# Two-layer encoder trunk on one Trainium2 core: PSUM bank order, placing of the adaLN dots, of the norm products, and the pairing in the MLP head's second half

## The chip, the cores and the metric

The kernel runs on one core of one Trainium2 chip. The metric is device time in microseconds (us), as the median over runs. Engines go by the profile's names: PE (TensorE matmuls; PEld its weight loads), DVE (VectorE), ACT (ScalarE), POOL (GpSimd) and SP (SyncE, whose queue issues the transfers).

## What is computed

Two residual layers over x of shape (512, 1024). Each layer modulates an RMS norm by adaLN, runs a mixer, adds it back with a gate, and does the same with an MLP.

```python
for layer in range(DEPTH):
    mod = c_act @ ada_w[layer] + ada_b[layer]
    shift1, scale1, gate1, shift2, scale2, gate2 = jnp.split(mod[:, None, :], 6, axis=-1)
    h = rms_norm(x, norm_mix[layer]) * (1.0 + scale1) + shift1
    y = mixer_conv_hgrn(h, ...) if layer % 2 == 0 else mixer_stick_breaking(h, ...)
    x = x + gate1 * y
    h = rms_norm(x, norm_mlp[layer]) * (1.0 + scale2) + shift2
    x = x + gate2 * (jnp.square(jax.nn.relu(h @ mlp_w1[layer])) @ mlp_w2[layer])
```

The mixer of layer 0 is a gated convolution beside a gated linear recurrence (HGRN2); that of layer 1 is stick-breaking attention with 16 heads. D_MODEL is 1024, D_FF is 4096. `mod` is a product of one vector with a 1024 x 6144 matrix for each layer.

## The kernel before, in words

**Layout.** x is kept transposed, as eight tiles x0 to x7 of 128 features x 512 positions. A "half" is 256 positions (`H[0]`, `H[1]`).

**Products.** Every f32 weight tile (128 x 1024, 512 KB) is loaded by SP into `wraw` or `raw`, a ring of three buffers, then split into a high part `whi` (ACT, L271; in the planned stage L1365) and a low part `wlo` (DVE, L272; L1366). `whi` and `wlo` have four slots each. The input h is likewise kept as `hh` and `hl`, the MLP's hidden values as `hidh` and `hidl`. `mm3` (L281 to L283) then makes one triple of matmuls: whi x hh, whi x hl, wlo x hh. Eight triples, k = 0 to 7, make one output tile.

**adaLN dots.** `mod` isn't made on PE: `ada_piece` loads one 512 KB tile through the same ring of three buffers, and `ada_dot` (L420) is one DVE instruction that multiplies it with the broadcast c and sums each row into a column of `modr`. The elementwise product, which nobody reads, goes to a scratch tile `ascr` in bf16. Sixteen dots are made at the start; the other 80 wait in a list, `todo`, and `background(n)` takes the next n. Calls of it stand after the v and g products (4), after each of four `lin` products (2), in and after each of four convolutions (3 + 2), and in the blocks of the first MLP (`PIECES`: 3, 3, 3, 3, 2 for block 0, 3, 3, 2, 2, 2 for blocks 1 and 2, and 2 each for block 3, behind outputs 0 to 4).

**PSUM.** Up to the output projection of layer 0, pool `mps` holds `acc` (four banks), `lv` (two) and `misc` (two). Then it is closed, and pool `pp` has eight tiles b0 to b7 that take the banks over. `acc()` of that pool goes round them and begins with b4. A tag gets its place in the pool when it is first named, so before the change b4 lies on bank 0, b5 on bank 1 and so on round.

**Order of work in layer 0.** PE's order is the program's; the order of DVE, ACT and SP is set by the framework from priorities and estimated times. The output projection runs outputs 0 to 2 together, then 3, then 4 to 7 by halves. `x_add` (L506) adds an output to x, `nrm.add` adds the square to `nss`; the norm of a half (`finish`) sums `nss` and the last square over partitions by matmuls with a tile of ones (L497), takes the root (Ln, Exp and one Newton step on DVE) and writes eight h tiles, each by DVE, ACT, DVE (L466 to L468). Then comes the **MLP head** (`mlp_head`): hidden tiles 0 to 3 by halves. `first()` makes four outputs of half 0 with two banks (b4, b5), k outermost; `second(j)` makes half 1 one output after the other. `sums` prepares the inputs of the block products, on DVE and ACT. Four blocks follow, each with pairs of hidden tiles (`pair`), then outputs (`second`, `products`, `done`): 5 or 8 output tiles of eight triples each.

**Order of work from the end of MLP 0 to the head of MLP 1.** Here a planner (`Graph`) sets the order of PE, DVE, ACT and SP. Each operation has an estimated duration and a priority. The planner takes the earliest possible start, and among operations that can start then, the lowest priority number, then the one created first. Its engines start at time 0. Norm work has priority 0, triples and weight splits have 1. `finish` there (L1396) issues the sum by matmuls with ones (L1399), Ln and Exp (L1402, L1403), the Newton step (L1404 to L1406) and the h tiles (L1410 DVE, L1412 ACT, L1414 DVE). `NormTasks.add` makes the squares (ACT, L1385) and adds them to `nss` (DVE, L1389). All triples are held in the order of the list `order`. The three places with halves are: the tail of MLP 0 (outputs 5 to 7, 24 triples a half) followed by the q and k products of two head pairs (32 triples a half); and the last part of the attention's output projection (24 triples a half) followed by the head of MLP 1 (32 triples a half). `mean_squares` (L1452) sums the squares of q and k, which `q_evict` and `k_evict` make on ACT (L1426, L1443).

The choice of the planner, in its own words:

```python
t0 = min(t for t, o in at)
t, o = min(((t, o) for t, o in at if t <= t0 + self.tol), key=lambda c: (c[1].prio, c[1].seq))
```

Of the kernel before, what the change touches and what calls it, by code (L numbers as in the profile page):

```python
# [25 lines left out]
NT = 8  # L26
# [194 lines left out]
def trunk(tc, x_d, c_d, rep_d, small_d, const_d, ada_d, ws_d, win_d, wv_d, woab_d, w1_d, w2_d, wqk_d, wvc_d, woc_d, out_d):  # L221
# [53 lines left out]
    def load_w(src, of=None, at=AT512):  # L275
        return split_w(raw_w(src), of, at)
# [140 lines left out]
    def ada_dot(l, v, f, raw):  # L417
        scr = adap.tile([P, 1024], BF16, name="ascr", tag="ascr", bufs=1)
        col = l * 48 + v * 8 + f
        dve.tensor_tensor_reduce(out=scr, in0=raw, in1=cb, scale=1.0, scalar=0.0, op0=ALU.mult, op1=ALU.add,  # L420
                                 accum_out=modr[:, col:col + 1])
# [26 lines left out]
    def background(n):  # L448
        for _ in range(min(n, len(todo))):
            l, v, f = todo.pop(0)  # L450
            ada_piece(l, v, f)
            if f == 7:
                ada_done(l, v, 0, 8)
# [470 lines left out]
    for h in range(4):  # L924
        run(lin(h, do_hg, h))
        background(2)


    def conv(i):
# [19 lines left out]
        y[i] = (yh, yl)  # L949
        background(2)  # L950

# [21 lines left out]
    PLACES = {5: (mp, "F2", "Q2"), 6: (mp, "Ft", "Kt")}  # L973
    run(proj((0, 1, 2), [load_w(woab_d[o]) for o in (0, 1, 2)], FULL))
    for o in range(3, HALVED[0]):
        run(proj((o,), [load_w(woab_d[o])], FULL))
    ws = {o: load_w(woab_d[o], PLACES.get(o), AT256) for o in HALVED}
    for hf in range(2):
# [11 lines left out]

    pp = pool("pp", PSUM)

    bank = [4]
# [140 lines left out]

    PIECES = ((3, 3, 3, 3, 2), (3, 3, 2, 2, 2), (3, 3, 2, 2, 2), (2, 2, 2, 2, 2))

    def mlp(l, last, hp, head, th, more=()):
# [3 lines left out]
        for b in range(4):  # L1141
# [14 lines left out]
            def done(o, ps):  # L1156
                x_add(o, ps, FULL, l, GATE2)
                if b == 3:
                    if last:
                        sync.dma_start(out_d[o], x[o])  # L1160
                    else:
                        nrm.add(o, FULL)
                if o < 5:
                    background(PIECES[b][o])

            p0 = second(0)
            products(p0, 0, 7)
            rest()
            p1 = second(1)
            products(p1, 0, 7)  # L1170
# [26 lines left out]
    def mlp_head(l, nin, hp):  # L1197
# [21 lines left out]

        def second(j):  # L1220
            ps = acc(256)
            for k in range(NT):
                mm3(ps, w[j], ks(k), hT[k], H[1], k == 0, k == NT - 1)
                yield 0.32
            evict(j, ps, H[1])

        run(first())
        flush()
        more = []
        for j in range(4):  # L1230
            run(second(j))
            if j < 2:
                more.append(load_w(w1_d[l, 4 + j]))
            if j == 1:
                th = [[Handle(t=hp.tile([P, 1088], F32R, name=f"t{i}{a}", tag=f"t{i}{a}")[:, AT512]) for a in "hl"] for i in range(4)]
                sums(l, th, lambda eng, n, fn, r, w: fn())
# [156 lines left out]

    def finish(parts, hf, l, which, table, at=-9.0):

        sl, ps, a, y = H[hf], miscs.new(), nass.new(), nys.new()  # L1396

        for i, q in enumerate(parts):
            on_pe(0.44, lambda i=i, q=q: pe.matmul(ps.t[:, :256], ones, q.t[:, sl], start=(i == 0), stop=(i == len(parts) - 1)),  # L1399
                  (q,), (ps,), 0, at=at)  # L1400
        m = lambda: ps.t[:, :256]
# [223 lines left out]
    for hf in range(2):  # L1625
        for o in range(5, 8):
            order += [mm3h(tail[o, hf], whole, w_tail[o - 5], ks(k), (hid[k],), H[hf], k == 0, k == 7, 256) for k in range(8)]
            on_dve(310, lambda o=o, hf=hf: x_add(o, tail[o, hf].t, H[hf], 0, GATE2), (tail[o, hf], xh[o, hf]), (xh[o, hf],), 0)
            nt_.add(o, hf)
        if hf:  # L1630
            gate = G.op("HOST", 0.0, open_attention, after=[order[-1]])
            for r in ap_rings:
                r.gate = gate
        finish([nt_.acc[hf]] + [nt_.sq[o, hf] for o in nin.direct], hf, 1, 0, ())
    w = [weights(wqk_d[s // 2, s % 2], None, AT256) for s in range(4)]
    for hf in range(2):
        ps = [r.new() for r in (accs, accs, zts, zts)]
        for k, s in by_half(hf, 4):
# [23 lines left out]
    nt_ = NormTasks((5, 6, 7))  # L1662
    for hf in range(2):
        order += wout(2, hf, wl, nt_)
        if hf == 0:
            hh = h_parts([[ring(base, [P, T], F32R, f"h{a}{i}").new() for a in "hl"] for i in range(NT)])
        finish([nt_.acc[hf]] + [nt_.sq[o, hf] for o in nt_.direct], hf, 1, 1, table)

# [24 lines left out]

    w = [weights(w1_d[1, j], None, AT256) for j in range(4)]
    for hf, sl in enumerate(H):

        ps = [accs.new() for _ in range(2)] if hf == 0 else [zts.new() for _ in range(4)]
        ps = [(ps[j // 2], lambda t_, j=j: t_[:, H[j % 2]]) if hf == 0 else (ps[j], half) for j in range(4)]
        for k, j in by_half(hf, 4):
            order.append(mm3h(*ps[j], w[j], ks(k), (hh[hf][k],), sl, k == 0 and (hf == 1 or j % 2 == 0), k == NT - 1, 256))  # L1700
# [94 lines left out]
```

## Time and profile before

| | |
|---|---|
| median of three runs | 1259.93 us (1259.74 to 1262.07) |
| the profiled execution, its own time | 1268.89 us |
| its span | 1267.1 us |
| mean granted PE clock | 0.986 |
| busy: PE / DVE / ACT | 1231.2 / 891.7 / 619.1 us |
| read from HBM | 155.96 MB |

The profile is one execution. Busy times are unions of instructions on an engine. A row of the timeline gives start, length, engine, line, what is written from what, and in brackets the idle time before it with what ended that. A granted clock below 1 in a stretch means that for a part of it PE ran at a lower clock; (1 - clock) x length is the time lost if PE had work throughout.

### The profile page before, as it was taken

The numbers are of one execution on the slowest core, as the hardware profiler recorded it, in microseconds if no ns is written. First come the engines' busy times: TensorE is split into PE (matmuls) and PEld (weight loads), VectorE is DVE, ScalarE is ACT, GpSimd is POOL, SyncE is SP. The second block draws the span as 40 slices with busy tenths as digits, with TensorE's granted clock in tenths as the row PEclk, the third lists the DMA queues.
The fourth block names the chain that finished last, engine by engine and source line by source line (L and its number), as shares of the span: only waits on it lengthen the run. The fifth ranks groups of instructions, "written<-read, shape, count | busy, mean of one in ns | idle before, by whom it ended". The sixth has DMA issues, their size and how long they took to land.

```text
span 1267.1 us, 19222 instructions
## 1 busy us (share of the span) xinstructions
PE 1231.2 (97%) x7649; PEld 1066.7 (84%) x7649; DVE 891.7 (70%) x1435; ACT 619.1 (49%) x1111; POOL 13.8 (1%) x24
## 2 busy tenths in 40 slices
PE   8999999999999999999999999999989999999998
PEld 6788777889779799798878787778888898898998
DVE  8897777659768787787657774668786574675661
ACT  4333133337238256264447763667565274372560
POOL 0000000000000000000120000000000000000000
PEclk9999899999999999999989999999989999999999
DMA  8666544312743735626413212231113224243141
GB/s 302 243 212 216 165 166 134 133 35 89 253 140 126 255 119 177 222 98 219 167 37 97 84 51 83 85 100 67 51 47 104 100 85 132 67 148 102 51 151 50
DMA packets 46618, 163.50 MB, mean 129 GB/s; under 512 B 5296, under 2 KB 6328, under 8 KB 46528
## 3 DMA queue, kind: packets, MB, share of 16 engines
q1 hardware_dynamic: 46384, 161.78, 38.7%
q8 instruction: 60, 0.98, 0.3%
q10 hardware_dynamic: 144, 0.49, 0.1%
q14 instruction: 30, 0.25, 0.1%
HBM read 155.96 MB, written 2.10 MB: 125 GB/s over the span
## 4 chain that ended last, share of the span: by engine, by line
PE 73%; DVE 11%; DMA 9%; ACT 4%; issue 2%; SPq 0%; ACTq 0%; DVEq 0%
PE b L281 17%; PE b L283 17%; PE b L282 17%; DMA wraw<-in_w 4%; PE acc L281 3%; PE acc L282 3%; PE acc L283 3%; DVE wlo L272 3%; DVE ascr L420 2%; DMA wraw<-in_ada 2%; ACT whi L271 2%; PE b L1532 1%; PE b L1553 1%; PE b L1588 1%; PE b L1452 1%
## 5 line engine op out<-in xcount | busy, mean ns | idle before, releaser
L271 ACT CAST whi<-wraw 128x1024 fp32r<-128x1024 f32 x125 | 130.2, 1049 | 235.0 <-DMA wraw<-in_w 78.0
L281 PE MATMUL b<-hidh,whi 128*128 128x512 f32 (+1 forms) x560 | 210.3, 376 | 4.4 <-ACT whi L271 4.4
L283 PE MATMUL b<-hidh,wlo 128*128 128x512 f32 (+1 forms) x560 | 210.0, 375 | 2.4 <-DVE wlo L272 2.4
L282 PE MATMUL b<-hidl,whi 128*128 128x512 f32 (+1 forms) x560 | 209.4, 374 | 0.0
L281 PE MATMUL b<-hh,whi 128*128 128x256 f32 (+1 forms) x632 | 198.3, 314 | 3.6 <-DVE x L506 2.9
L272 DVE TENSOR_TENSOR wlo<-wraw,whi 128x1024 fp32r<-128x1024 f32 x125 | 152.0, 1221 | 60.9 <-ACT whi L271 59.1
L283 PE MATMUL b<-hh,wlo 128*128 128x256 f32 (+1 forms) x632 | 193.6, 306 | 0.3 <-DVE wlo L272 0.3
L282 PE MATMUL b<-hl,whi 128*128 128x256 f32 (+1 forms) x632 | 193.2, 306 | 0.0
L281 PEld LDWEIGHTS b<-hh,whi 128*128 128x128 f32 x632 | 120.8, 191 | 16.3 <-issue 7.2
L281 PEld LDWEIGHTS b<-hidh,whi 128*128 128x128 f32 x560 | 106.3, 190 | 24.0 <-ACT whi L271 6.1
L506 DVE SCALAR_TENSOR_TENSOR x<-b,modc,x 128x512 f32<-128x512 f32 (+1 forms) x102 | 67.9, 673 | 83.1 <-PE b L283 82.9
L282 PEld LDWEIGHTS b<-hl,whi 128*128 128x128 f32 x632 | 122.6, 194 | 4.5
L283 PEld LDWEIGHTS b<-hidh,wlo 128*128 128x128 f32 x560 | 106.0, 189 | 24.1 <-DVE wlo L272 5.4
L283 PEld LDWEIGHTS b<-hh,wlo 128*128 128x128 f32 x632 | 120.9, 191 | 5.8 <-DVE wlo L272 0.5
L282 PEld LDWEIGHTS b<-hidl,whi 128*128 128x128 f32 x560 | 106.5, 190 | 18.4 <-DVE hidl L291 0.3
L420 DVE CUSTOM_DVE_ANT_0 ascr<-wraw,cb 128x1024 bf16<-128x1024 f32 x80 | 97.8, 1222 | 27.2 <-DMA wraw<-in_ada 26.5
L272 DVE TENSOR_TENSOR wlo<-tt,whi 128x1024 fp32r<-128x1024 f32 x52 | 63.3, 1220 | 28.6 <-ACT whi L271 28.0
L271 ACT CAST whi<-tt 128x1024 fp32r<-128x1024 f32 x52 | 53.4, 1050 | 44.1 <-PE b L282 30.4
L1366 DVE TENSOR_TENSOR wlo<-raw,whi 128x1024 fp32r<-128x1024 f32 x34 | 41.5, 1221 | 24.7 <-ACT whi L1365 24.5
L291 DVE TENSOR_TENSOR hidl<-cm,hidh 128x256 fp32r<-128x256 f32 (+1 forms) x90 | 44.5, 509 | 17.1 <-ACT hidh L290 16.1
L281 PE MATMUL acc<-hh,whi 128*128 128x512 f32 x128 | 53.2, 416 | 0.0
L282 PE MATMUL acc<-hl,whi 128*128 128x512 f32 x128 | 50.9, 398 | 0.0
(378 smaller groups left out, 2642.4 us busy)
## 6 DMA issues: line engine op xcount, KB each, us to landing
wraw<-in_w SPq DMA_DIRECT2D x124, 512.0 KB, 3.7
wraw<-in_ada SPq DMA_DIRECT2D x80, 512.0 KB, 4.4
eraw<-in_ada SPq DMA_DIRECT2D x16, 512.0 KB, 4.1
wraw<-in_win SPq DMA_DIRECT2D x16, 512.0 KB, 4.2
raw<-in_wqk SPq DMA_DIRECT2D x16, 512.0 KB, 3.7
raw<-in_ws SPq DMA_DIRECT2D x8, 512.0 KB, 6.9
wraw<-in_woab SPq DMA_DIRECT2D x8, 512.0 KB, 3.3
raw<-in_wvc SPq DMA_DIRECT2D x8, 512.0 KB, 4.3
```

What stands on the lines that cost most here:

```text
L271: act.copy(hi, raw)
L272: dve.tensor_tensor(lo, raw, hi.bitcast(F32), op=ALU.subtract)
L281: pe.matmul(ps, whi, h[0][:, hs], start=start, stop=False, **kw)
L282: pe.matmul(ps, whi, h[1][:, hs], start=False, stop=False, **kw)
L283: pe.matmul(ps, wlo, h[0][:, hs], start=False, stop=stop, **kw)
L291: dve.tensor_tensor(lo[:, sl], t_[:, sl], hi[:, sl].bitcast(F32), op=ALU.subtract)
L420: dve.tensor_tensor_reduce(out=scr, in0=raw, in1=cb, scale=1.0, scalar=0.0, op0=ALU.mult, op1=ALU.add, accum_out=modr[:, col:col + 1])
L506: dve.scalar_tensor_tensor(x[o][:, sl], ps, mcol(l, v, o), x[o][:, sl], op0=ALU.mult, op1=ALU.add)
L1366: on_dve(1024, lambda: dve.tensor_tensor(lo.t, raw.t, hi.t.bitcast(F32), op=ALU.subtract), (raw, hi), (lo,), 1)
L1452: on_pe(0.13, lambda s=s, sq=sqs[p, s, s0]: pe.matmul(ms.t[64 + 32 * s:96 + 32 * s, sl], hs, sq.t[:, sl], start=True, stop=True), (sqs[p, ...
L1532: pe.transpose(tp.t[:, o_:o_ + P], be.t[:, w0:w0 + P], ident)
L1553: pe.matmul(po.t[orow, P * b - t0:P * (b + 1) - t0], v.t[:, c, hcol], be.t[:, w0:w0 + P], start=first[j], stop=(c == b), skip_group_check= ...
```

## The change

Five edits.

1. `ada_dot` writes its product over the weight tile itself; the scratch tile `ascr` is gone.
2. The 80 dots are placed anew: one instead of two after each `lin` product and after each convolution, two each at three places around the first four outputs of the output projection, two in the MLP head, and `PIECES` in six entries of 2 or 3, the first of which stands between the first and the second output weight of a block.
3. b0 to b7 are named in order when pool `pp` is opened, so b4 lies on bank 4.
4. The head's second half makes two outputs at a time, in both layers.
5. In the planner, `finish` is created later, and its first matmul waits for a set triple of `order` (ninth of the second half, sixth of the second half, or ninth of what follows).

```diff
     def ada_dot(l, v, f, raw):
-        scr = adap.tile([P, 1024], BF16, name="ascr", tag="ascr", bufs=1)
         col = l * 48 + v * 8 + f
-        dve.tensor_tensor_reduce(out=scr, in0=raw, in1=cb, scale=1.0, scalar=0.0, op0=ALU.mult, op1=ALU.add,
+        dve.tensor_tensor_reduce(out=raw, in0=raw, in1=cb, scale=1.0, scalar=0.0, op0=ALU.mult, op1=ALU.add,
                                  accum_out=modr[:, col:col + 1])
...
         run(lin(h, do_hg, h))
-        background(2)
+        background(1)
...
         y[i] = (yh, yl)
-        background(2)
+        background(1)
...
-    run(proj((0, 1, 2), [load_w(woab_d[o]) for o in (0, 1, 2)], FULL))
+    w = [load_w(woab_d[o]) for o in (0, 1, 2)]
+    background(2)
+    run(proj((0, 1, 2), w, FULL))
+    background(2)
     for o in range(3, HALVED[0]):
         run(proj((o,), [load_w(woab_d[o])], FULL))
+        background(2)
...
     pp = pool("pp", PSUM)
+    for b in range(8):
+        pp.tile([P, T], F32, name=f"b{b}", tag=f"b{b}")
...
-    PIECES = ((3, 3, 3, 3, 2), (3, 3, 2, 2, 2), (3, 3, 2, 2, 2), (2, 2, 2, 2, 2))
+    PIECES = ((2, 2, 3, 2, 2, 2), (2, 2, 3, 2, 2, 2), (2, 2, 2, 2, 2, 2), (2, 2, 2, 2, 2))
...
-                if o < 5:
+                if 0 < o < len(PIECES[b]):
                     background(PIECES[b][o])
...
             products(p0, 0, 7)
             rest()
+            background(PIECES[b][0])
             p1 = second(1)
...
-        def second(j):
-            ps = acc(256)
+        def second(js):
+            ps = [acc(256) for _ in js]
             for k in range(NT):
-                mm3(ps, w[j], ks(k), hT[k], H[1], k == 0, k == NT - 1)
-                yield 0.32
-            evict(j, ps, H[1])
+                for p_, j in zip(ps, js):
+                    mm3(p_, w[j], ks(k), hT[k], H[1], k == 0, k == NT - 1)
+                yield 0.64
+            for p_, j in zip(ps, js):
+                evict(j, p_, H[1])
 
         run(first())
+        background(2)
         flush()
-        more = []
-        for j in range(4):
-            run(second(j))
-            if j < 2:
-                more.append(load_w(w1_d[l, 4 + j]))
-            if j == 1:
+        for js in ((0, 1), (2, 3)):
+            run(second(js))
+            if 0 in js:
+                more = [load_w(w1_d[l, j]) for j in (4, 5)]
...
-    def finish(parts, hf, l, which, table, at=-9.0):
+    def finish(parts, hf, l, which, table, after=()):
...
-                  (q,), (ps,), 0, at=at)
+                  (q,), (ps,), 0, after=after if i == 0 else ())
...
-        if hf:
-            gate = G.op("HOST", 0.0, open_attention, after=[order[-1]])
-            for r in ap_rings:
-                r.gate = gate
-        finish([nt_.acc[hf]] + [nt_.sq[o, hf] for o in nin.direct], hf, 1, 0, ())
+    gate = G.op("HOST", 0.0, open_attention, after=[order[-1]])
+    for r in ap_rings:
+        r.gate = gate
+
+    finish([nt_.acc[0]] + [nt_.sq[o, 0] for o in nin.direct], 0, 1, 0, (), [order[24 + 8]])
     w = [weights(wqk_d[s // 2, s % 2], None, AT256) for s in range(4)]
     for hf in range(2):
+        if hf:
+            finish([nt_.acc[1]] + [nt_.sq[o, 1] for o in nin.direct], 1, 1, 0, (), [order[48 + 8]])
...
-    for hf in range(2):
-        order += wout(2, hf, wl, nt_)
-        if hf == 0:
-            hh = h_parts([[ring(base, [P, T], F32R, f"h{a}{i}").new() for a in "hl"] for i in range(NT)])
-        finish([nt_.acc[hf]] + [nt_.sq[o, hf] for o in nt_.direct], hf, 1, 1, table)
+    order += wout(2, 0, wl, nt_)
+    hh, at = h_parts([[ring(base, [P, T], F32R, f"h{a}{i}").new() for a in "hl"] for i in range(NT)]), len(order)
+    order += wout(2, 1, wl, nt_)
+    finish([nt_.acc[0]] + [nt_.sq[o, 0] for o in nt_.direct], 0, 1, 1, table, [order[at + 5]])
...
-    w = [weights(w1_d[1, j], None, AT256) for j in range(4)]
+    w, at = [weights(w1_d[1, j], None, AT256) for j in range(4)], len(order)
     for hf, sl in enumerate(H):
+        if hf:
+            finish([nt_.acc[1]] + [nt_.sq[o, 1] for o in nt_.direct], 1, 1, 1, (), [order[at + 8]])
...
-        for k, j in by_half(hf, 4):
+
+        for k, j in by_half(0, 4) if hf == 0 else [(k, j) for js in ((0, 1), (2, 3)) for k in range(NT) for j in js]:
             order.append(mm3h(*ps[j], w[j], ks(k), (hh[hf][k],), sl, k == 0 and (hf == 1 or j % 2 == 0), k == NT - 1, 256))
```

## The prediction, made before the result was known

> **What bounds the kernel now.** I read the page first, for the engine that the span hangs on.
>
> ```profile
> span 1267.1 us, 19222 instructions
> PE 1231.2 (97%) x7649; PEld 1066.7 (84%) x7649; DVE 891.7 (70%) x1435; ACT 619.1 (49%) x1111; POOL 13.8 (1%) x24
> PEclk9999899999999999999989999999989999999999
> ```
>
> TensorE is busy for 97%, so an edit pays only where PE stands still or runs at a lower granted clock. I looked for such places in the busy times by stretch. Columns: stretch, its length, busy time of PE, PEld, DVE, ACT and POOL, granted clock, DMA share, GB/s.
>
> ```profile
> 143.00:154.00 11.00, 9.20 (x39) 7.60 (x38) 9.78 (x17) 1.04 (x1) 0.00 (x0) 0.69 0.52 161
> 225.00:250.00 25.00, 25.00 (x122) 21.10 (x121) 15.26 (x18) 11.57 (x13) 0.00 (x0) 1.00 0.43 147
> 271.00:280.00 9.00, 5.86 (x31) 5.23 (x31) 4.86 (x11) 2.78 (x6) 0.00 (x0) 0.81 0.18 58
> 280.00:310.00 30.00, 30.00 (x215) 28.23 (x213) 28.66 (x54) 22.93 (x47) 0.00 (x0) 1.00 0.15 44
> 335.00:360.00 25.00, 20.58 (x79) 15.24 (x78) 16.02 (x21) 6.29 (x6) 0.00 (x0) 0.93 0.73 243
> 432.00:436.00 4.00, 3.21 (x14) 2.02 (x13) 2.37 (x3) 1.05 (x1) 0.00 (x0) 1.00 0.62 217
> 518.00:522.00 4.00, 2.47 (x10) 1.39 (x10) 2.55 (x4) 1.04 (x1) 0.00 (x0) 1.00 0.45 154
> 617.00:625.00 8.00, 5.08 (x28) 4.70 (x27) 3.04 (x6) 1.96 (x4) 0.00 (x0) 0.79 0.43 136
> 643.00:660.00 17.00, 14.01 (x64) 10.41 (x64) 9.77 (x24) 9.20 (x24) 0.00 (x0) 0.70 0.05 11
> 917.00:929.00 12.00, 7.42 (x39) 6.53 (x39) 8.22 (x20) 4.49 (x11) 0.00 (x0) 0.72 0.14 44
> ```
>
> Each row gives two losses: length less PE busy, and (1 - clock) x length. They are 1.8 + 3.4 us at 143, 3.1 + 1.7 at 271, 4.4 + 1.8 at 335, 0.8 at 432, 1.5 at 518, 2.9 + 1.7 at 617, 3.0 + 5.1 at 643 and 4.6 + 3.4 at 917: together 39 us, 22 of idle time and 17 of clock. That is nearly all that this change can win. The rows 225:250 and 280:310 show none.
>
> [...]
>
> **The change part by part.** Two prices are used throughout: the pace of the three-matmul products.
>
> ```profile
> 236.01 0.39 PE L281 MATMUL acc<-yy,whi 128*128 128x512 f32 x1
> 236.69 0.39 PE L281 MATMUL acc<-yy,whi 128*128 128x512 f32 x1
> 617.27 0.28 PE L283 MATMUL b<-hidh,wlo 128*128 128x256 f32 x1
> 617.63 0.28 PE L283 MATMUL b<-hidh,wlo 128*128 128x256 f32 x1
> ```
>
> A triple of 512 columns takes 0.68 us and one of 256 takes 0.36, so an output tile of eight triples takes 5.4 or 2.8 us.
>
> *Dots in place* (L420). The instruction keeps its place and inputs; its output becomes f32 and overwrites the weight tile.
>
> ```profile
> L420 DVE CUSTOM_DVE_ANT_0 ascr<-wraw,cb 128x1024 bf16<-128x1024 f32 x14 | 17.1, 1221 | 2.6 <-DMA wraw<-in_ada 2.4
> L272 DVE TENSOR_TENSOR wlo<-wraw,whi 128x1024 fp32r<-128x1024 f32 x5 | 6.1, 1225 | 6.4 <-ACT whi L271 6.4
> L271 ACT CAST whi<-wraw 128x1024 fp32r<-128x1024 f32 x5 | 5.3, 1051 | 20.3 <-DMA wraw<-in_w 18.4 <-PE b L282 1.9
> wraw<-in_ada SPq DMA_DIRECT2D x14, 512.0 KB, 4.4
> wraw<-in_w SPq DMA_DIRECT2D x7, 512.0 KB, 4.7
> ```
>
> (Groups and DMA issues of 308 to 350.) The bf16 dot takes 1221 ns, a subtraction with a full-width output 1225. Cost 0; even 4 ns on all 80 dots is 0.3 us, beside PE.
>
> *Dots, ahead of the first MLP.* Two instead of one, fewer by eight up to the last convolution; six more behind the output projections, two in the head.
>
> ```profile
> 142.38 1.23 DVE L420 CUSTOM_DVE_ANT_0 ascr<-wraw,cb 128x1024 bf16<-128x1024 f32 x1 [2.24 <-DMA wraw<-in_ada]
> 145.49 0.74 PE L808 MATMUL lv<-Q,Kt 128*128 128x64 f32 x5 [1.80 <-DVE Kt L839]
> ```
>
> At 143 PE waits for a DVE product that stands behind a dot, and that dot waited 2.24 us for its transfer. With 24 dots instead of 32 in this stage, the three weight buffers come round sooner. The loss is 5.2 us; I take 4.2 as won (bounds 0 and 5.2), nearer to the upper end because one dot less at 1.2 us plus its transfer nearly covers the 2.24. The six moved dots (7.3 us of DVE and their six transfers on SP) lie under the 25 us of 225:250, where PE never waits, DVE has 9.7 us free and DMA is 0.43 busy; cost 0. Without that cover they would cost up to their 7.3 us. The two in the head land where DVE is full (28.66 of 30): I charge 0.5 us, with bounds 0 (they fit ahead of 281, where the 271 row has DVE idle for 4.1 of 9) and 2.4 (both delay the weight splits behind them one for one).
>
> *Dots of the four MLP blocks.* From 308 to 350, 14 + 7 tiles pass through three buffers in 42 us: 2.0 us a tile. Before, six dots stand between the second and third output weight, 12 us of queue, then three per output: four tiles, 8.0 us, against 5.4 us of products. That is the stall at 335, with ACT idle for 18.4 us on weight transfers. Now two dots go in ahead of the second weight and two to three follow each: three tiles are 6.0 us. The deficit per output falls from 2.6 to 0.6 us over five outputs, and the third weight's queue shortens by four tiles, 8 us. So the 6.2 + 0.8 + 1.5 = 8.5 us go but for 1.0: 7.5 won (bounds 4 and 8.5). Queued behind the earlier dots is the second weight itself, by 4 us; before it comes the whole seven-triple run on the first, 4.8 us.
>
> *Banks named in order* (b0 to b7 on banks 0 to 7). The head's first two accumulators leave the projection's banks.
>
> ```profile
> 271.13 1.05 ACT L271 CAST whi<-wraw 128x1024 fp32r<-128x1024 f32 x1
> 274.65 1.21 DVE L272 TENSOR_TENSOR wlo<-wraw,whi 128x1024 fp32r<-128x1024 f32 x1
> 274.78 0.39 PE L281 MATMUL b<-hh,whi 128*128 128x256 f32 x1 [2.86 <-DVE x L506]
> 275.91 0.38 PE L283 MATMUL b<-hh,wlo 128*128 128x256 f32 x1 [0.27 <-DVE wlo L272]
> ```
>
> The 2.86 us wait on `x` (L506) disappears. But the fourth head weight's low half is ready only at 275.9, DVE working through the norm before it, and the fourth product of k = 0 needs it. PE would run one more triple and wait for that. Won: 0 (upper bound 4.8, the row's loss; a loss has no mechanism, since the new banks are long free).
>
> *Head's second half by two.* The same 32 triples; each k lasts 0.7 us instead of 0.36, so the last tile of h is asked for 2.5 us later. PE has no idle time in 280:310, so nothing is won; the pairwise evictions come at most 2.8 us later, and the casts of the next weights with them, ahead of a use 5.6 us on. Cost 0 (bounds -0.3 and 0.5).
>
> *Norm products behind a set number of others.* Three places. The planner takes, of ready operations, the lower priority and then the earlier created; `finish` is now created behind the second half's additions to x, so these also go ahead of its h tiles on DVE.
>
> ```profile
> 617.84 1.23 DVE L1366 TENSOR_TENSOR wlo<-raw,whi 128x1024 fp32r<-128x1024 f32 x1 [0.67 <-ACT whi L1365]
> 620.34 0.43 DVE L1389 TENSOR_TENSOR nss<-nss,nsq 128x256 f32<-128x256 f32 x1 [0.54 <-ACT nsq L1385]
> 620.82 1.12 PE L1399 MATMUL b<-nss,ones 128*128 128x256 f32 x2 [2.92 <-DVE nss L1389]
> 629.50 1.67 DVE L1410 SCALAR_TENSOR_TENSOR tt<-x,gsc,ny 128x256 f32<-128x256 f32 x4
> 635.85 0.41 DVE L1389 TENSOR_TENSOR nss<-nss,nsq 128x256 f32<-128x256 f32 x1
> 646.22 0.39 ACT L1443 ACTIVATE nsq<-b 128x256 f32<-128x256 f32 x1
> 646.67 0.90 PE L1452 MATMUL b<-nsq,cons 128*32 128x256 f32 x4 [2.24 <-ACT nsq L1443]
> ```
>
> At 617.9 one triple of the first half is left. Ten triples, 3.6 us, now come before the sum, so PE reaches it at 621.5, behind 620.8. Won: 2.9 + 1.7 less 0.5 for the first h tile, about 4.1 (bounds 0 and 4.6). The sum's chain then starts some 3 us earlier against PE. Queued behind the sum's matmul is the rest of the tail; it no longer stands.
>
> At 643, PE waits for evictions that share ACT with the second half's h tiles. These were late because the second sum stood behind eight pairs of h instructions (629.5 to 635.9) on DVE. With the additions first, that sum can go behind nine projection triples, some 4 us earlier against PE; the h tiles (eight times 0.8 us) end about when the first half's 32 triples (11.4 us) do. Of 8.1 us I take 7.0 (bounds 0 and 8.1).
>
> ```profile
> 912.72 1.05 ACT L1365 CAST whi<-raw 128x1024 fp32r<-128x1024 f32 x1 [0.21 <-PE b L282]
> 921.10 0.41 DVE L1389 TENSOR_TENSOR nss<-nss,nsq 128x256 f32<-128x256 f32 x1
> 923.84 1.19 PE L1399 MATMUL b<-nss,ones 128*128 128x256 f32 x2 [4.58 <-DVE nss L1389]
> 924.01 1.21 DVE L1366 TENSOR_TENSOR wlo<-raw,whi 128x1024 fp32r<-128x1024 f32 x1
> ```
>
> At 917 the sum comes off PE's way, but behind it stands the same kind of split as in layer 0: the fourth weight's low half, of lower priority than all the norm's work on DVE, ends at 925.2. The fourth triple needs it. Won: 1.0 (bounds 0 and 8.0).
>
> **Sum**: 4.2 + 7.5 + 0 + 4.1 + 7.0 + 1.0 - 0.5 = 23.3 us. The profiled execution took 1268.89 us (span 1267.1 and 1.8 around it), so 1245.6. The median of the three runs is 1259.93, 0.7% less; the same share off gives 1236.8, so 1237.
>
> **The rivals.**
> 1. *The fourth weight is split early* (chance 0.16). Its cast is done at 913.8, in the gaps of the norm's short chain; a planner that takes the earliest start may slip it in there. Then 917 gives 7 us more and, likewise, 271 up to 4.8: 1225 to 1230. Against it: both rows show it last.
> 2. *The sums still block PE* (0.15). The plan starts DVE at time 0, but in the trace it was still splitting at 617.84; if `nss` is really later than planned, PE stands at the set place instead. The 11.1 us of 617 and 643 are lost: 1248.
> 3. *The clock dips stay* (0.07), having another cause than idle time. Only idle time is won: about 12 us, 1248. Every dip in the rows lies on idle time, which speaks against it. [...]
> 4. *Dots only trade places* (0.03), the transfers as late as now at 143 and 335 and the norms as in 2: under 1 us, 1259.5, no change.
> 5. *Slower* (0.07). [...]
>
> **How the numbers follow.** The forecast has 0.52, with a range of its own of 1230 to 1246. Faster by over 0.2% (2.5 us, about what a measurement of this kernel tells from no change): forecast and rivals 1 to 3, 0.90. Same 0.03, slower 0.07. The range from 1224 to 1253 takes in rivals 1 to 3 and the bounds of the MLP term, and leaves out the last two.
>
> **What would show it.** PE waits on `nss` gone or under 1 us in all; no granted clock below 0.9 around 617 and 643; the wait on `x` (L506) replaced by one on `wlo` (L272) of like length; ACT's wait for `in_w` transfers in the first MLP block under 8 us; no wait of PE on `Kt`. I am wrong if 271 or 917 become free of loss (rival 1), or if PE waits on `nss` at 621 or 631 for more than 2 us (rival 2).

## The result, and the profile after

The changed kernel takes 1246.03 us in the median, the kernel before beside it 1260.08 us: a ratio of 0.9883, with a 95% interval of 0.9864 to 0.9902. The 1246.03 is the median of four executions, one of which was slow (1502.91 us at a mean clock of 0.75); the other three took 1245.21, 1245.68 and 1246.37 us. Compared once more, the changed kernel took 1245.42 us, with the kernel before at 1264.02 beside it: a ratio of 0.9856 (0.9833 to 0.988). It is faster by 14 to 19 us in the medians. The forecast of 1237 lies 9 us too low, within its range of 1224 to 1253.

The two ratios are of one and the same kernel and differ by 0.0027, which is 3.4 us. So where two runs below differ by no more than that, their times don't settle which is faster; what an edit does at its place is then read from the traces.

The profiled execution of the changed kernel took 1245.21 us. The page, as for the kernel before:

```profile
span 1243.4 us, 19173 instructions
PE 1217.4 (98%) x7649; PEld 1058.9 (85%) x7649; DVE 890.5 (72%) x1435; ACT 618.7 (50%) x1111; POOL 11.2 (1%) x24
PEclk9999999999999999999999999999999999999999
```

All three slices at 8 are gone, and PE is busy for 13.8 us less with the same 7649 matmuls: fewer of them ran at a lower clock (its mean is 0.996, where it was 0.986). From profile to profile the span falls by 23.7 us, which is almost the forecast's 23.3; the medians differ by 14. The experiments settle what lies between.

The same stretches of work in the changed kernel, by the busy times in stretches (columns as in the prediction). The times have moved with the gain; the order is that of 143, 271, 335, 432, 518, 617, 643, the head of MLP 1 and its end.

```profile
141.00:152.00 11.00, 11.00 (x73) 9.86 (x71) 10.67 (x19) 2.28 (x3) 0.10 (x1) 1.00 0.34 108
264.00:273.00 9.00, 5.81 (x31) 5.28 (x30) 4.54 (x10) 2.69 (x6) 0.00 (x0) 0.81 0.17 58
327.00:345.00 18.00, 18.00 (x82) 14.88 (x80) 13.28 (x21) 3.16 (x3) 0.00 (x0) 1.00 0.74 239
416.00:420.00 4.00, 4.00 (x20) 3.30 (x19) 1.92 (x4) 0.00 (x0) 0.00 (x0) 1.00 0.80 252
500.00:504.00 4.00, 4.00 (x19) 3.30 (x19) 2.31 (x5) 1.05 (x1) 0.00 (x0) 1.00 0.86 294
598.00:606.00 8.00, 8.00 (x67) 7.89 (x66) 5.67 (x10) 5.51 (x10) 0.00 (x0) 1.00 0.42 137
621.00:638.00 17.00, 16.78 (x113) 12.47 (x111) 9.84 (x27) 10.98 (x28) 0.00 (x0) 1.00 0.32 91
889.00:901.00 12.00, 9.37 (x58) 8.77 (x57) 8.03 (x21) 5.13 (x13) 0.00 (x0) 0.86 0.02 8
917.00:929.00 12.00, 8.04 (x38) 6.53 (x38) 9.03 (x13) 5.86 (x11) 0.00 (x0) 0.86 0.26 88
```

Five of the nine rows are now full and a sixth (621) is so but for 0.2 us, all six at full clock. The row at 264 is as bad as it was, and the head of MLP 1 has two bad rows where it had one. PE's waits over the whole span name the tiles:

```profile
PE b L283 <- DVE wlo L272: 7.1, 2, 4.0
PE acc L651 <- ACT hh L640: 3.3, 3, 2.3
PE b L281 <- ACT hh L1419: 2.0, 1, 2.0
...
PE b L282 <- DVE hl L1421: 1.2, 2, 0.7
...
PE lv L807 <- DVE Kt L838: 1.0, 2, 0.5
...
PE b L281 <- DVE x L505: 0.2, 1, 0.2
```

No wait on `nss` is left (7.5 us before). The waits on `wlo`, 3.2 and 4.0 us, and on the `hh` of L1419 with the `hl` behind it are the new ends of the line (the `hh` of L640 belongs to the kernel's start, and was 4.3 us before). A bracket counts from the modelled end of a matmul. The expectations below count a gap from about where the next matmul would have started at the pace before it (a third of the triple: 0.12 us behind the last start for 256 columns, 0.23 for 512), which is an estimate of mine. So the 3.19 us of `wlo` is 3.36 there, the 3.96 is 4.1, and the 1.97 us on `hh` and 0.66 on `hl` in the last head are 2.14 and 0.93. Where the waits come from, in the timeline of PE and of DVE:

```profile
265.13 0.28 PE L282 MATMUL b<-hl,whi 128*128 128x256 f32 x1
268.60 0.57 PE L283 MATMUL b<-hh,wlo 128*128 128x256 f32 x1 [3.19 <-DVE wlo L272]
...
919.20 0.40 PE L282 MATMUL b<-hl,whi 128*128 128x512 f32 x1
923.56 0.50 PE L283 MATMUL b<-hh,wlo 128*128 128x512 f32 x1 [3.96 <-DVE wlo L272]
```

```profile
265.81 0.87 DVE L467 SCALAR_TENSOR_TENSOR hl<-tt,modc,hh 128x256 fp32r<-128x256 f32 x2
266.60 0.41 DVE L490 TENSOR_TENSOR nss<-nss,nsq 128x256 f32<-128x256 f32 x1
266.94 0.47 DVE L505 SCALAR_TENSOR_TENSOR x<-acc,modc,x 128x256 f32<-128x256 f32 x1
267.33 1.21 DVE L272 TENSOR_TENSOR wlo<-wraw,whi 128x1024 fp32r<-128x1024 f32 x1
...
885.27 1.22 DVE L1373 TENSOR_TENSOR wlo<-raw,whi 128x1024 fp32r<-128x1024 f32 x1
...
887.53 0.42 DVE L1411 SCALAR_TENSOR_TENSOR na<-b,ny 128x256 f32<-128x256 f32 x1
...
889.37 0.42 DVE L1412 TENSOR_TENSOR na<-na,ny 128x256 f32<-128x256 f32 x1
889.99 0.48 DVE L505 SCALAR_TENSOR_TENSOR x<-b,modc,x 128x256 f32<-128x256 f32 x1 [0.20 <-PE b L283]
890.39 0.41 DVE L1413 SCALAR_TENSOR_TENSOR ny<-na,ny 128x256 f32<-128x256 f32 x1
890.84 1.67 DVE L1417 SCALAR_TENSOR_TENSOR tt<-x,gsc,ny 128x256 f32<-128x256 f32 x4
...
920.48 1.22 DVE L1026 TENSOR_TENSOR t3l<-tt,t3h 128x1024 fp32r<-128x1024 f32 x1
921.61 0.75 DVE L1717 TENSOR_TENSOR hidl<-cm,hidh 128x256 fp32r<-128x256 f32 x2
922.28 3.49 DVE L272 TENSOR_TENSOR wlo<-wraw,whi 128x1024 fp32r<-128x1024 f32 x3
```

At 267 the fourth weight's split is last on DVE, as it was before. At 885 it is early, but the three Newton steps (L1411 to L1413) take from 887.5 to 890.8, additions to x and to `nss` standing between them. At 922 the first block's weight is split behind the last pair of hidden tiles.

To add this up, I set the start of the same matmul (the 600th, 800th and so on) in both traces side by side; what the difference grows by is the gain of that part. The second column does it for a repeated profile of each kernel (the first experiment below and the last but one).

| part | forecast, us | first two profiles | repeated profiles |
|---|---|---|---|
| first 600 matmuls | 0 | +1.9 | +0.2 |
| 143 | 4.2 | +5.4 | +2.8 |
| 271 | 0 | +0.6 | -1.6 |
| rest of the layer-0 head | -0.5 | -0.8 | -0.9 |
| four MLP blocks | 7.5 | +10.4 | +11.0 |
| 617 | 4.1 | +4.6 | +4.5 |
| 643 | 7.0 | +6.4 | +4.3 |
| head of MLP 1 and its end | 1.0 | -4.6 | -3.9 |
| sum (with 0 to -0.2 elsewhere) | 23.3 | 23.7 | 16.4 |

### The profile page after: what moved, and what is told of

It is laid out like the page before. It is cut to its first block, busy times and chain, and to the rows that moved or that the text cites. A ratio compares the mean times of both kernels' runs of the same rounds, so it can differ in the third digit from the quotient of the medians.

```text
span 1243.4 us, 19173 instructions
## 1 busy us (share of the span) xinstructions
PE 1217.4 (98%) x7649; PEld 1058.9 (85%) x7649; DVE 890.5 (72%) x1435; ACT 618.7 (50%) x1111; POOL 11.2 (1%) x24
## 4 chain that ended last, share of the span: by engine, by line
PE 84%; DVE 8%; DMA 4%; ACT 2%; issue 1%; SPq 0%; DVEq 0%; ACTq 0%
PE b L281 20%; PE b L283 20%; PE b L282 20%; PE acc L281 3%; PE acc L283 3%; PE acc L282 3%; PE b L1539 2%; PE b L1560 1%; DMA raw<-in_ws 1%; PE b L1595 1%; PE b L1459 1%; DMA wraw<-in_w 1%; PE b L1596 1%; PE b L1597 1%; DVE wlo L272 1%
## 5 line engine op out<-in xcount | busy, mean ns | idle before, releaser
L282 PE MATMUL b<-hidl,whi 128*128 128x512 f32 (+1 forms) x560 | 208.4, 372 | 1.0 <-DVE hidl L291 1.0
L282 PE MATMUL b<-hl,whi 128*128 128x256 f32 (+1 forms) x632 | 193.3, 306 | 1.2 <-DVE hl L1421 1.2
L272 DVE TENSOR_TENSOR wlo<-wraw,whi 128x1024 fp32r<-128x1024 f32 x125 | 152.1, 1222 | 58.8 <-ACT whi L271 57.6
L282 PEld LDWEIGHTS b<-hl,whi 128*128 128x128 f32 x632 | 121.8, 193 | 6.2 <-DVE hl L1421 1.8
L282 PEld LDWEIGHTS b<-hidl,whi 128*128 128x128 f32 x560 | 105.6, 188 | 19.5 <-DVE hidl L291 1.6
L419 DVE CUSTOM_DVE_ANT_0 wraw<-wraw,cb 128x1024 f32<-128x1024 f32 x80 | 97.4, 1221 | 26.3 <-DMA wraw<-in_ada 25.9
L272 DVE TENSOR_TENSOR wlo<-tt,whi 128x1024 fp32r<-128x1024 f32 x52 | 63.4, 1221 | 22.5 <-ACT whi L271 21.9
L1373 DVE TENSOR_TENSOR wlo<-raw,whi 128x1024 fp32r<-128x1024 f32 x34 | 41.6, 1222 | 23.6 <-ACT whi L1372 23.5
L291 DVE TENSOR_TENSOR hidl<-cm,hidh 128x256 fp32r<-128x256 f32 (+1 forms) x90 | 44.4, 510 | 18.5 <-ACT hidh L290 17.7
L1523 DVE TENSOR_TENSOR_SCAN om<-om,pat 128x772 f32<-128x772 f32 (+2 forms) x24 | 46.5, 1936 | 5.8 <-ACT om L1519 5.8
```

Source lines behind the costliest of these rows:

```text
L272: dve.tensor_tensor(lo, raw, hi.bitcast(F32), op=ALU.subtract)
L282: pe.matmul(ps, whi, h[1][:, hs], start=False, stop=False, **kw)
L291: dve.tensor_tensor(lo[:, sl], t_[:, sl], hi[:, sl].bitcast(F32), op=ALU.subtract)
L419: dve.tensor_tensor_reduce(out=raw, in0=raw, in1=cb, scale=1.0, scalar=0.0, op0=ALU.mult, op1=ALU.add, accum_out=modr[:, col:col + 1])
L1373: on_dve(1024, lambda: dve.tensor_tensor(lo.t, raw.t, hi.t.bitcast(F32), op=ALU.subtract), (raw, hi), (lo,), 1)
L1523: on_dve(2 * nw, lambda: dve.tensor_tensor_scan(s_(), s_(), pats[i][:, ::-1], 0.0, op0=ALU.mult, op1=ALU.max), (om,), (om,), 2)
```

## The experiments

**The kernel before once more**, without an edit.

> The unchanged kernel once more, with a profile of its own. Theory A (the losses are fixed by the program): the profile shows the same 39 us of loss in the eight places and a time near 1269 us, and the timed runs near 1260 because something in the runs without that profile is faster throughout. Theory B (the clock dips differ from one execution to the next): idle times repeat to 0.3 us, the lower granted clock does not, and the execution takes about 1260 us with some 9 us less lost to clock.

Measured: 1261.96 us against 1260.93, ratio 1.0014 (0.9995 to 1.0032). Its profiled execution took 1261.43 us, 7.5 less than the first one, with nearly the same idle gaps, but another clock:

```profile
141.00:152.00 11.00, 8.81 (x55) 7.31 (x54) 11.00 (x19) 1.04 (x1) 0.00 (x0) 1.00 0.50 156
267.00:276.00 9.00, 5.86 (x45) 5.35 (x44) 5.19 (x13) 3.58 (x7) 0.00 (x0) 1.00 0.19 58
```

At 141 and 267 PE stands at least as long as in the first profile (9.20 and 5.86 us busy there), but the clock is 1.00 where it was 0.69 and 0.81. By the mean clock, 0.986 of 1267.1 us and 0.990 of 1259.6, the lower clock cost 17.7 us in the first and 12.6 in this one. So 5 of the 7.5 us are clock; another 1.7 lie in the first 600 matmuls. That is theory B, with 5 of its 9 us, and the first profile showed a dearer execution than usual.

**The dots alone**: the kernel before with edits 1 and 2.

```diff
+    PIECES = ((2, 2, 3, 2, 2, 2), (2, 2, 3, 2, 2, 2), (2, 2, 2, 2, 2, 2), (2, 2, 2, 2, 2))
...
+            background(PIECES[b][0])
             p1 = second(1)
```

> The kernel before with the dots' edits alone (in place, spread by twos). My terms: 4.2 at 143 and 7.5 in the MLP blocks less 0.5 in the head, 11.2 us of profiled time; 617, 643 and 917 keep their losses. Rival (dots only trade places): under 1 us. If clock dips differ from run to run, the median gains less than the profile, 5 to 11 us.

Measured: 1249.11 us, ratio 0.9906 (0.9885 to 0.9927), 11.8 us less, where the terms gave 11.2. Against the repeated profile of before, the start of equal matmuls gives +2.8 at 143 and +10.2 over the four blocks, less 2.2 at 271 and in the layer-0 head. The dots carry most of the gain.

**The norm products alone**: the kernel before with edit 5.

```diff
+    finish([nt_.acc[0]] + [nt_.sq[o, 0] for o in nin.direct], 0, 1, 0, (), [order[24 + 8]])
```

> The kernel before with the planner's edit alone (norm products behind a set triple). My terms: 4.1 + 7.0 at 617 and 643 and about 1 to 8 at 917, 12 to 19 us of profiled time; 143, 271 and 335 keep theirs. With the head still one output after the other no wait on a weight's low half at the two whole tiles behind the head. Rival (the sums still block): under 4 us.

Measured: 1254.83 us, ratio 0.9941 (0.9919 to 0.9963), 6.1 us less, half of the 12 us or more that was expected. Equal matmuls give +4.8 at 617 and +4.8 at 643 (the terms: 4.1 and 7.0), but -1.6 in the head of MLP 1, where 1 to 8 had been counted on, and -2.3 at the layer-0 head, by the clock. PE's wait on `hh` stands in the head of MLP 1 here too:

```profile
PE b L281 <- ACT hh L1412: 2.3, 2, 2.0
```

So that wait belongs to this edit; the 4 us wait on the whole tile's `wlo` is not in this trace. One row of its profile shows the layer-0 head, which this edit doesn't touch:

```profile
269.00:278.00 9.00, 6.13 (x26) 5.57 (x25) 4.23 (x10) 2.23 (x5) 0.00 (x0) 0.63 0.19 58
```

PE stands for about as long as ever, and this time the clock is 0.63: the same gap at 1.00, 0.81 and 0.63 in three profiles.

**The last head by one**: the changed kernel with the second half of MLP 1's head one output at a time.

```diff
-        for k, j in by_half(0, 4) if hf == 0 else [(k, j) for js in ((0, 1), (2, 3)) for k in range(NT) for j in js]:
+        for k, j in by_half(hf, 4):
```

> The changed kernel with the second half of the second head one output after the other, as before. Theory: the 4.0 us wait of PE on a weight's low half behind that head comes from the pairing, which frees the first weights' slots one output later; without it that wait and its dip of the clock go, 4 to 6 us faster than the changed kernel, less up to 1.5 us if the last h tiles are now late. Rival (the wait comes from the planner's new order of the norm): no change within 1 us.

Measured: 1242.8 us, ratio 0.985 (0.9829 to 0.9871). PE is full at the head's end, and the short waits ahead of it are dearer (PE's waits from 880 to 925; the `hl` one is 1.2 us in the changed kernel):

```profile
914.00:926.00 12.00, 12.00 (x80) 11.04 (x80) 10.86 (x18) 7.62 (x14) 0.00 (x0) 0.99 0.25 86
```

```profile
PE b L281 <- ACT hh L1419: 2.3, 2, 2.0
PE b L282 <- DVE hl L1421: 2.2, 3, 0.8
```

The first split behind the head, in the changed kernel (ACT's high part) and one output at a time (DVE's low part):

```profile
915.93 1.06 ACT L271 CAST whi<-wraw 128x1024 fp32r<-128x1024 f32 x1
...
911.61 1.23 DVE L272 TENSOR_TENSOR wlo<-wraw,whi 128x1024 fp32r<-128x1024 f32 x1
```

The wait of 4.0 us is the pairing's. By pairs, the first weight behind the head is cast only at 915.93, and its low part on DVE, at 922.28, stands behind `sums` and the last two hidden tiles, which are evicted together at the very end. One at a time, the cast starts at 910.53, as soon as PE has left the slot, and the low part is done ahead of the last evictions and most of `sums`. In time the two kernels are too close for their ratios (0.985 against 0.9883 and 0.9856). By equal matmuls, the head and its end are 3.2 us shorter than in either profile of the changed kernel: 4.8 us won at the end, 1.6 lost ahead of it. The short waits there are 4.5 us in all, against 3.2; the clock was 0.87 from 902 to 914, which is 1.6 us, where the changed kernel had lost 1.7 from 889 to 901 (0.86).

**The banks as before**: the changed kernel without the naming loop.

```diff
-    for b in range(8):
-        pp.tile([P, T], F32, name=f"b{b}", tag=f"b{b}")
```

> The changed kernel without the lines that name the banks b0 to b7 in order; all else is as in the changed kernel. Theory A (the banks are worth nothing here, because the low half of the fourth head weight ends at the same time as the wait for the banks): the first triple of the head waits about 2.9 us on x (L505) again, the wait on wlo (L272) in its place is gone or under 0.5 us, and the time is within 1 us of the changed kernel. Theory B (the banks give part of the 4.8 us that this place lost before): 2 to 5 us slower than the changed kernel.

Measured: 1244.33 us, ratio 0.9877 (0.9853 to 0.9901). That is 1.7 and 1.1 us under the two medians of the changed kernel, so not slower: theory A, if not to the last word. The wait on `x` is back, and the one on `wlo` is down to 0.27 us:

```profile
267.87 0.39 PE L281 MATMUL b<-hh,whi 128*128 128x256 f32 x1 [2.87 <-DVE x L505]
...
269.00 0.43 PE L283 MATMUL b<-hh,wlo 128*128 128x256 f32 x1 [0.27 <-DVE wlo L272]
```

By equal matmuls this place takes as long as in the changed kernel, to 0.1 us.

**The fourth output late**: the changed kernel with the fourth output tile of the layer-0 head's first half behind the other three.

```diff
-            for k in range(NT):
-                for j in range(4):
-                    mm3(ps[j], w[j], ks(k), hT[k], H[0], k == 0 and j % 2 == 0, k == NT - 1, skip_group_check=True)
-                yield 1.28
+            for js in ((0, 1, 2), (3,)):
+                for k in range(NT):
+                    for j in js:
+                        mm3(ps[j], w[j], ks(k), hT[k], H[0], k == 0 and j % 2 == 0, k == NT - 1, skip_group_check=True)
+                    yield 0.32 * len(js)
```

> The changed kernel with one edit in the head of layer 0: in the first half, the fourth output tile runs behind the other three over all k, not beside them, so its weight's low half is asked for some 8.6 us later (24 triples of 0.36 us). Theory A (the wait moved from x to the low half, L272): PE's 3.36 us gap at 265 goes, and the 3.41 us at half clock behind it, so 3.4 to 5 us faster than the changed kernel. Theory B (something else is next late, such as the h tiles or the evictions of the projection): under 1 us faster, with a PE wait of 2 us or more on another tile between 262 and 280.

Measured: 1240.98 us, ratio 0.9854 (0.983 to 0.9877), 3.4 us less than the run with the banks as before in the same set. PE no longer stops in that stretch:

```profile
260.00:269.00 9.00, 8.80 (x69) 8.14 (x68) 7.78 (x20) 5.62 (x12) 0.00 (x0) 1.00 0.02 5
```

By equal matmuls the layer-0 head is 4.7 us shorter than in either profile of the changed kernel: theory A at its place. In the head of MLP 1, which the edit doesn't touch, this execution lost 2 us of that again; the clock was 0.76 from 911 to 923 there, where the changed kernel had 0.86 from 917 to 929, which is 1.2 us.

**The fourth output late, the banks as before**: both edits.

> The kernel of the run before it in this list (the fourth output of the layer-0 head behind the other three), without the lines that name the banks in order. Theory A (the banks take away a wait of their own that only the low half hid): PE waits about 2.9 us on x (L505) at 267, and the time is 2.5 to 5 us over that of the run with the banks in order. Theory B (the banks do nothing either way): within 1 us of it.

Measured: 1242.38 us, ratio 0.9863 (0.9839 to 0.9887). The wait is back in the trace:

```profile
266.97 0.58 PE L281 MATMUL b<-hh,whi 128*128 128x256 f32 x1 [2.86 <-DVE x L505]
```

That the banks take away a wait which the split hides is shown by the trace. The time, 1.4 us over the run with the banks in order, is under the 2.5 that theory A set, and the intervals overlap: what the banks give is not settled by it. Equal matmuls tell why: the layer-0 head is 3.4 us longer than with the banks in order, with the 2.86 us wait and a clock of 0.81 from 263 to 272, 1.7 us, while the head of MLP 1, which the banks don't touch, took 3.6 us less in this execution. The mean clock of the whole is 0.996 here and 0.994 with the banks in order.

**The Newton steps first**: the two edits that helped, and the planner's priority of L1411 to L1413 from 0 to -1.

```diff
-        on_dve(256, lambda: dve.tensor_tensor(a.t, a.t, y.t, op=ALU.mult), (y, a), (a,), 0)
+        on_dve(256, lambda: dve.tensor_tensor(a.t, a.t, y.t, op=ALU.mult), (y, a), (a,), -1)
```

> The changed kernel with three edits: the second half of the last head one output at a time as before, the fourth output of the layer-0 head behind the other three, and the three DVE steps of the norm's inverse root (L1411 to L1413) ahead of every other ready DVE operation of the planner. Theory A (the hh waits of 2.1 + 0.9 us in the last head come from these steps standing behind additions to x): the hh waits fall under 1 us in all, and with the 4.0 us of the whole hidden tile and the 3.4 to 5 us of the layer-0 head also gone the time is 1233 to 1239. Theory B (hh is late by the length of the chain itself): the hh waits stay at 3 us, and the time is 1237 to 1241, as the other two edits alone would give.

Measured: 1235.52 us, ratio 0.981 (0.9784 to 0.9836). The time is theory A's, the wait is not: the part on `hh` fell from 1.97 to 1.51 us only, and the 0.66 us on `hl` behind it stayed. So the time is in part luck: the head of MLP 1 and its end are 1.9 us shorter by equal matmuls than in the last head by one, and beyond the 0.5 us of the wait that is mostly clock: 0.87 from 902 to 914 in that execution, 1.6 us, and 1.00 from 896 to 908 in this one. The Newton steps now end at 882.5, but before the h tiles stand four additions to x and two to `nss`:

```profile
882.10 0.41 DVE L1414 SCALAR_TENSOR_TENSOR ny<-na,ny 128x256 f32<-128x256 f32 x1
882.43 0.87 DVE L505 SCALAR_TENSOR_TENSOR x<-b,modc,x 128x256 f32<-128x256 f32 x2
883.22 0.41 DVE L1397 TENSOR_TENSOR nss<-nss,nsq 128x256 f32<-128x256 f32 x1
883.55 0.48 DVE L505 SCALAR_TENSOR_TENSOR x<-b,modc,x 128x256 f32<-128x256 f32 x1
883.95 0.41 DVE L1397 TENSOR_TENSOR nss<-nss,nsq 128x256 f32<-128x256 f32 x1
884.28 0.48 DVE L505 SCALAR_TENSOR_TENSOR x<-b,modc,x 128x256 f32<-128x256 f32 x1
884.68 1.66 DVE L1418 SCALAR_TENSOR_TENSOR tt<-x,gsc,ny 128x256 f32<-128x256 f32 x4
```

Neither theory holds as it was put: the steps were late, but what stands between them and the h tiles made up most of the wait.

**The h tiles first**: also the DVE steps of the last norm's h tiles at -1.

```diff
-                   op0=ALU.mult, op1=ALU.mult), (xh[i, hf], y), (t_,), 0)
+                   op0=ALU.mult, op1=ALU.mult), (xh[i, hf], y), (t_,), -which)
```

> The kernel with the three edits (second half of the last head by one, the fourth output of the layer-0 head behind the other three, the Newton steps first), and a fourth: the DVE steps of the h tiles of the last norm (L1417 and L1421) also ahead of every other ready DVE operation. Theory A (the h tiles in the last head are late because additions to x, the nss additions and the MLP's own steps stand before them): the 1.7 + 0.9 us gaps at the head's start go to under 1 us in all, the 1.1 + 1.0 us on hl in its second half too, and the time is 3 to 4.5 us under the kernel with three edits, 1231 to 1233. Theory B (what is put behind them, the sum of the second half, is late next): a wait on nss or nsq of 1.5 us or more, and the time within 1.5 us of the kernel with three edits.

Measured: 1236.15 us, ratio 0.9783 (0.9766 to 0.9801). The head's start is nearly free; the second half of the head pays:

```profile
880.00:892.00 12.00, 11.41 (x95) 11.03 (x94) 10.12 (x27) 5.43 (x13) 0.00 (x0) 1.00 0.14 44
894.00:906.00 12.00, 9.54 (x55) 8.44 (x54) 11.93 (x28) 8.98 (x23) 0.00 (x0) 0.77 0.00 0
```

The first row had 9.83 us busy in the run before: the wait on `hh` is gone there, and 0.59 us on `hl` is left. The second half has waits on `hh` and `hl` of 0.5 to 0.9 us each, 2.3 in all, where the run before had 1.9 (10.02 of 12 us busy, at a clock of 1.00). DVE is full there in both, 11.93 and 11.97 of 12 us. Theory A's cause is shown for the head's start, its gain isn't: of the 1.6 us won there, the next half, where DVE has no room, took back 0.5, and a lower clock more than the rest (0.77 over 12 us, 2.8 us, which the run before was spared). The two versions cannot be told apart; both are 9 to 11 us under the changed kernel and 24 to 28 under the kernel before.

**The changed kernel once more**, without an edit.

> The changed kernel, unchanged. Theory A (the idle gaps belong to the program, the stretches at a lower granted clock only in part): the same waits of PE as in the first profile of it to within 0.5 us each, among them 3.4 us on the low half (L272) at 265 and 4.1 us at 919, while at least one of the half-clock stretches behind them differs in length or is gone. Theory B (the stretches belong to the program too): the same three stretches of 3.41 us. The time is within 3 us of 1246.

Measured: 1245.42 us, ratio 0.9856 (0.9833 to 0.988). The waits repeat (3.18 us at 265, 2.0 at 890, 3.73 at 919), and so does the clock around the first and the last of them: 0.81 from 264 to 273 and 0.86 from 917 to 929, as in the first profile. That by itself would be theory B. For theory A speak two other pairs. The kernel before has the same 2.86 us gap at the layer-0 head in both its profiles, at 0.81 in one and at 1.00 in the other. And the run with the banks as before has the 2.0 us on `hh` and the 3.9 on `wlo` in the last head too, but a mean clock of 0.997, where the changed kernel's two profiles have 0.996 and 0.995. So I take the stretches to be chance in part; two profiles of the changed kernel alone don't settle it.

**The layer-0 head by one**: the changed kernel with that head's second half one output at a time.

```diff
-        for js in ((0, 1), (2, 3)):
-            run(second(js))
+        for j in range(4):
+            run(second((j,)))
```

> The changed kernel with one edit: the second half of the layer-0 head makes one output at a time, as before the change; the pairing in the head of layer 1 stays. Theory A (the pairing costs nothing in layer 0, since no wait of PE hangs on it there): the time is within 1 us of the changed kernel. Theory B (the pairing costs here what it costs in layer 1): 3 to 5 us faster than the changed kernel.

Measured: 1245.78 us, ratio 0.9859 (0.9833 to 0.9884), beside 1245.42 for the changed kernel in the same set: theory A. (The weight loads and `sums` of the head stand as before the change, too.) By equal matmuls the layer-0 head is 0.5 to 0.6 us shorter one at a time, so the pairing is nearly free where no wait hangs on it.

## Why the prediction was right, and where it was off

- **Dots in place, right.** A dot takes 1221 ns in the mean of the 80, and took 1222 before.
- **143, right.** The `Kt` wait fell from 1.8 us at the most to 0.5. The part gave 5.4 and 2.8 us around the forecast's 4.2; the spread is the clock's, which before the change was 0.69 over 11 us in one profile (3.4 us) and 1.00 in the other.
- **MLP blocks, right in the mechanism, too small.** PE waits for nothing from 325 to 350. The term was 7.5, with an upper bound of 8.5; it measured 10.4 and 11.0. The three places were all there was: the profile has 6.75 us of idle time in the blocks, and 6.7 was counted. What was too small is the price of a wait. One of the nine:

```profile
345.09 0.50 PE L281 MATMUL b<-hidh,whi 128*128 128x512 f32 x1 [1.97 <-ACT whi L271]
```

By the starts of equal matmuls this wait set PE back by 2.24 us, 0.27 more than its bracket, since busy time runs to a modelled end. Nine such waits make 2.5 us. With the 1.0 us that I had left standing, and that went as well, this is what was missing; the first profile of the changed kernel has a new wait of 0.74 us on `hidl` at 567, which the second has not. One sign that I had named was wrong: ACT's wait for weight transfers did not fall under 8 us.

```profile
ACT whi L271 <- DMA wraw<-in_w: 17.0, 4, 5.8
```

ACT waits nearly as long as before (18.4). I take it that what counted was how far ahead of PE it did so; no run tests that by itself.

- **Banks, right.** Won nothing, as forecast: the wait moved from `x` to `wlo`, at 3.2 us instead of 2.9; the runs with the banks as before and with the fourth output late show both halves of it.
- **617 and 643, right.** 11.0 and 8.8 us against 11.1; rival 2 (the sums still block PE) fell with the last wait on `nss`.
- **Head of MLP 1, wrong.** The step that failed is "behind it stands the same kind of split as in layer 0: the fourth weight's low half". It was split early, at 885.27, as rival 1 had it, but without rival 1's gain: `hh` and `hl` were late next, 2.6 us of waits, because `finish`, created later, lost its place on DVE to the additions to x and `nss`. The Newton steps first took back 0.5 us of it, the h tiles first all but 0.6. I had noted that order at 643, where it helps the second sum, and not asked what it does to the first half's Newton steps and h tiles here.
- **Pairing, wrong for layer 1.** "Cost 0" was worked out from the layer-0 rows at 280:310 alone, where it holds. In layer 1 the same edit cost a wait of 4.0 us and, at a clock of 0.50 for 3.41 us (924.00 to 927.41), 1.7 more. The last head by one took back 3.2 us by equal matmuls.
- **From the profile to the median, wrong.** "The same share off" took the sum nearly whole, 22.9 us, from a median execution. But it was read off one that lost 17.7 us to the clock, where the repeat lost 12.6. By equal matmuls 2.6 us of the difference between the two lie at 143 and 1.6 at 643, in gaps that the change removes, and 2.2 at 271, in one that it leaves. Against the repeated profiles the sum is 6.9 us too large: 1.4 at 143, 1.6 at 271 and 2.7 at 643, for the most part clock (before, 1.00 at 143 and 0.80 at 643 in the repeat, 0.69 and 0.70 in the first; at 271, 1.00 before and 0.81 after), and 4.9 in the head of MLP 1, less 3.5 in the blocks and small ones elsewhere. 1260.1 less 16.4 is 1243.7, which lies in the measured interval (1242.9 to 1247.7); the last 2.3 us to 1246.03 stay open. That the forecast's 23.3 us and the 23.7 between the first two profiles nearly agree is luck: blocks too small, head of MLP 1 too large, and a dear first execution.
- **Rivals 3, 4 and 5 fell.** The dots alone gave 11.8 us. The clock dips went with the gaps: at 143, 335, 617 and 643 it was 0.69, 0.93, 0.79 and 0.70, and is 1.00 at all four. For rival 5 no run shows a reason: the kernel is faster, and the second products of layer 0 and 1 take as long as ever (372 ns in the mean for L282 over 560, 374 before).

## What to carry to other kernels

A wait that is taken away shows the next late thing, and that must be looked for at every place where an edit acts: the same pairing was nearly free in one layer and brought a wait of 4 us in the other, where the next product needs a weight that is split behind the last eviction. Moving an operation's creation in a planner that breaks ties by age moves all its followers behind what is now older. And a profile's lost clock is partly luck (17.7 and 12.6 us in two executions of the kernel before): profile the kernel before twice, count a wait by the starts of the matmuls around it, and take gains in idle time as firmer than those in clock, which are a range.

## What the runs showed of the hardware

One gap of the layer-0 head, nearly the same in seven profiles, did not come with one clock. The waits are the brackets of the timeline, or the length of the stretch less PE's busy time; the clock is the mean over 9 us around them, and the last column is (1 - clock) x 9 us.

| profile | PE's waits there, us | stretch | granted clock | time lost to it, us |
|---|---|---|---|---|
| before, first | 2.86 + 0.27 | 271:280 | 0.81 | 1.7 |
| before, again | 2.86 + 0.28 | 267:276 | 1.00 | 0 |
| norm products alone | 2.87 | 269:278 | 0.63 | 3.3 |
| after, first | 3.19 | 264:273 | 0.81 | 1.7 |
| after, again | 3.18 | 264:273 | 0.81 | 1.7 |
| banks as before | 2.87 + 0.27 | 263.5:272.5 | 0.82 | 1.6 |
| fourth output late, banks as before | 2.86 | 263:272 | 0.81 | 1.7 |
| fourth output late | 0.2 in all | 260:269 | 1.00 | 0 |

In the first profile of the changed kernel the lower clock is one stretch at 0.50, from 268.64 to 272.05, which begins with the matmuls behind the wait. So a gap of about 3 us came without any lower clock in one execution, with 1.6 to 1.7 us lost to it in five, and with 3.3 in one; where the gap was taken away but for 0.2 us, the clock was 1.00. What decides between these is not shown by the runs.
